# A transformer layer on one core: the second token half is scaled for four tiles at once, turned chunk pair by chunk pair, and the second weight pair's sums move to the end of the turns

## The chip, the core and the metric

The kernel runs on one core of a Trainium2 chip. The metric is device time in microseconds (us) of one execution; a lower time is better. The engines are TensorE (PE in the profile, with PEld for its weight loads), VectorE (DVE), ScalarE (ACT), GpSimd (POOL) and SyncE (SP), whose queue issues the DMA transfers.

## The reference

One layer works on a token block `x` of 1024 tokens by 1024 features, in fp32:

```python
h = _rmsnorm(x, ffn1_norm[i]);  x = x + 0.5 * _swiglu(h, ffn1_w1[i], ffn1_w3[i], ffn1_w2[i])
h = _rmsnorm(x, mix_norm[i]);   proj = h @ w_in[i]      # q, f, v, output gate, pool, two branch gates
...                             # a chunked gated recurrence, a causal multi-scale pool, two branches
y = sigmoid(ga_r) * y_a + sigmoid(gb_r) * y_b;          x = x + y @ w_out[i]
h = _rmsnorm(x, ffn2_norm[i]);  x = x + 0.5 * _swiglu(h, ffn2_w1[i], ffn2_w3[i], ffn2_w2[i])
gate = sigmoid(_rmsnorm(x, ple_norm[i]) @ ple_w_gate[i]);  x = x + gate * e
return _rmsnorm(x, final_norm)
```

Three of the four large stages begin in the same way: all 1024 tokens are normalised, their features are brought onto the partitions, and a wide weight matrix multiplies them (`w1` and `w3` of both feed-forward blocks, and `w_in`). The fourth normalisation belongs to the gate at the end (PLE below).

## The kernel before

**Products.** fp32 operands are split into a high and a low fp32r part: the high part is a cast on ScalarE, the low part a subtraction on VectorE (`split`, L118 and L119). A product of two such operands is three matmuls into one PSUM bank (`mm3`, L157 to L159). A large product is cut into 2 by 2 blocks (token halves on one side, weight halves on the other) and done with seven block products instead of eight. `pair` does this for two weight blocks `wa` and `wb`: products 1 and 2 need only the first token half (B11 and B21, tiles x0h, x0l), product 3 needs B22 (the tile `x`, high and low in one), and products 5, 6 and 7 need T1, T2 and T3 (tiles xT1h, xT1l, xT3h, xT3l), sums of both halves. A block product has 4 chunks of 128 features, so 12 matmuls of 128x512.

On the weight side, `sums` builds S1 to S4 and A22. Four operations on GpSimd do it (L90 and three of L93), with casts on ScalarE and subtractions on VectorE between them: wsh, wsl for S1 and S2; wd for A22; wth, wtl for S3 and S4. The fourth GpSimd operation overwrites the tile `rb`, so it waits until wd has read it.

**The second token half.** `norm_act` brings a stage's tokens onto the partitions. `first` and `second` do it for tiles 0 to 3 and 4 to 7. In `second`, `scales` forms 1/rms of each token: two squares with row sums on ScalarE for each tile (L242), their sum on VectorE (L243), a power on GpSimd (L244) and a diagonal 128x128 matrix on VectorE (L245). This chain is run tile by tile. A *turn* of one chunk is four matmuls against these diagonals into one bank (L255): scaling and transposition in one. Then come the gain (L293, ScalarE) and the split of an odd chunk, and `act_second` (L198, L199, two subtractions L84, casts and subtractions) for a pair of chunks, which makes one chunk of T1, T2, T3 and N4.

In `second` all four odd chunks are turned first, which gives all of B22. Only then the four even chunks follow, each with its `act_second`.

**Leads.** At the start of a stage, `run_pair` collects three weight pairs (the *leads*, 0 to 2) and steps through them and through `second` in a written-out order, so that products 1 and 2 of three pairs and product 3 of two pairs cover the turns. `late` puts a pair's sums behind its products 1 and 2 instead of ahead of them (with a second load of `wa` as `ra`). Each engine takes its instructions strictly in its queue's order. That order is made once, ahead of time, by a scheduler from the order of the code and what depends on what; `tc.issue_after` holds following instructions back behind a given one.

The stages that start this way are FFN1 (its turns fall into about 20 to 70 us of the profile), the mix projection (about 713 to 752 us), and FFN2 (about 1656 to 1705 us). The PLE gate (about 2327 to 2336 us) uses `scales` too. In FFN1 the order is simpler (`begun` is empty): all of `second` runs between the products 1 and 2 of lead 1 and those of lead 2, with the products of the embedding projection (pw, L683) between the chunk pairs.

## Time and profile before

| | before |
|---|---|
| median of 3 runs | 2416.18 us (2415.89 to 2421.88) |
| the profiled execution's own time | 2417.04 us |
| its span, first to last instruction | 2415.3 us |
| mean granted TensorE clock | 0.990 |
| TensorE busy | 2330.6 us, 96% |
| VectorE, ScalarE, GpSimd busy | 1471.4, 980.0, 444.8 us |
| DMA, mean over the span | 137 GB/s |

A row of the timeline gives the start and the duration in us, the engine, the line, the operation, out<-in, how many instructions are in the row, and, in brackets, how long the engine was idle ahead of it and what released it. Matmuls overlap, so the distance between two starts, not the duration, is what one costs. A turn is a pass of eight (x8), since each fp32 matmul is recorded as two. A row of the windows gives a stretch of the span, its length, and for each engine named the busy time and the number of instructions; PEclk is the granted clock as a share of full speed.

### The profile page before, as it was taken

The numbers are of one execution on the slowest core, as the hardware profiler recorded it, in microseconds if no ns is written. First come the engines' busy times: TensorE is split into PE (matmuls) and PEld (weight loads), VectorE is DVE, ScalarE is ACT, GpSimd is POOL, SyncE is SP. The second block draws the span as 40 slices with busy tenths as digits, with TensorE's granted clock in tenths as the row PEclk, the third lists the DMA queues.
The fourth block names the chain that finished last, engine by engine and source line by source line (L and its number), as shares of the span: only waits on it lengthen the run. The fifth ranks groups of instructions, "written<-read, shape, count | busy, mean of one in ns | idle before, by whom it ended". The sixth has DMA issues, their size and how long they took to land. (4 is left out here: it accounts for less than half of the span.)

```text
span 2415.3 us, 29471 instructions
## 1 busy us (share of the span) xinstructions
PE 2330.6 (96%) x11058; PEld 1916.1 (79%) x11058; DVE 1471.4 (61%) x2037; ACT 980.0 (41%) x1528; POOL 444.8 (18%) x397
## 2 busy tenths in 40 slices
PE   8999999999998999999999999999899999999997
PEld 6778888888877888788888877877687888888886
DVE  6555554567656766766566566676544544568568
ACT  6344333333554333333333343237333333334556
POOL 1332223200011222122222102102222222100000
PEclk9999999999999999999999999999999999999999
DMA  4344453484332232222222257652234533663334
GB/s 183 127 143 168 156 174 132 153 322 128 117 114 70 79 96 83 75 88 79 83 81 86 88 189 247 229 207 105 87 129 146 177 102 110 215 251 127 97 100 152
DMA packets 133759, 331.75 MB, mean 137 GB/s; under 512 B 15216, under 2 KB 16240, under 8 KB 133616
## 3 DMA queue, kind: packets, MB, share of 16 engines
q1 hardware_dynamic: 133616, 329.87, 40.1%
q8 instruction: 87, 1.43, 0.3%
q14 instruction: 56, 0.46, 0.1%
HBM read 228.62 MB, written 101.19 MB: 137 GB/s over the span
## 5 line engine op out<-in xcount | busy, mean ns | idle before, releaser
L90 POOL TENSOR_TENSOR s<-rb 128x512 f32<-128x512 f32 x74 | 98.5, 1331 | 780.1 <-DMA rb<-in_ffn_w_dram 352.6
L119 DVE TENSOR_TENSOR wtl<-rb,wth 128x1024 fp32r<-128x1024 f32 x74 | 90.7, 1225 | 152.7 <-ACT wth L118 152.7
L118 ACT CAST wsh<-s 128x1024 fp32r<-128x1024 f32 x74 | 77.8, 1052 | 229.6 <-POOL s L93 215.5
L119 DVE TENSOR_TENSOR wsl<-s,wsh 128x1024 fp32r<-128x1024 f32 x74 | 91.3, 1233 | 117.9 <-ACT wsh L118 117.9
L93 POOL TENSOR_TENSOR rb<-ra,s 128x512 f32<-128x512 f32 x74 | 96.7, 1306 | 349.0 <-DVE wd L119 335.6
L118 ACT CAST wth<-rb 128x1024 fp32r<-128x1024 f32 x74 | 77.7, 1049 | 183.8 <-POOL rb L93 183.8
L954 PEld LDWEIGHTS aux<-qk 128*128 128x128 f32 (+1 forms) x896 | 109.7, 186 | 37.9 <-issue 11.5
L118 ACT CAST gh<-gr 128x1024 fp32r<-128x1024 f32 x84 | 81.8, 980 | 141.8 <-PE aux L158 86.4
L119 DVE TENSOR_TENSOR wal<-ra,wah 128x1024 fp32r<-128x1024 f32 x74 | 91.5, 1238 | 75.1 <-PE pC L158 45.0
L119 DVE TENSOR_TENSOR gl<-gr,gh 128x1024 fp32r<-128x1024 f32 x84 | 95.0, 1134 | 68.2 <-ACT gh L118 68.1
L157 PE MATMUL pA<-xT3h,wth 128*128 128x512 f32 x296 | 119.7, 404 | 8.9 <-ACT g L382 6.8
L954 PE MATMUL aux<-qk 128*128 128x64 f32 (+1 forms) x896 | 110.5, 267 | 17.2 <-DVE qk L87 11.5
L118 ACT CAST wah<-ra 128x1024 fp32r<-128x1024 f32 x74 | 77.6, 1050 | 117.6 <-DMA ra<-in_ffn_w_dram 97.2
L157 PE MATMUL pA<-xT1h,wsh 128*128 128x512 f32 x280 | 114.1, 408 | 10.4 <-ACT xT1h L118 7.1
L157 PE MATMUL pB<-xT1h,wsh 128*128 128x512 f32 x296 | 119.3, 403 | 2.6 <-DVE g L81 1.3
L157 PE MATMUL pA<-x0h,wah 128*128 128x512 f32 x296 | 118.5, 400 | 1.2 <-DVE gb L87 0.7
L157 PE MATMUL pC<-x0h,wah 128*128 128x512 f32 x296 | 118.9, 402 | 0.0
L157 PE MATMUL pB<-x,wth 128*128 128x512 f32 x296 | 118.8, 401 | 0.0
L158 PE MATMUL pA<-x0l,wah 128*128 128x512 f32 x296 | 115.8, 391 | 1.6 <-DVE x0l L119 1.6
L158 PE MATMUL pB<-xT1l,wsh 128*128 128x512 f32 x296 | 116.6, 394 | 0.8 <-DVE xT1l L119 0.8
L157 PE MATMUL pA<-xT3h,wd 128*128 128x512 f32 x280 | 112.8, 403 | 4.3 <-ACT c L385 2.5
L159 PE MATMUL pA<-xT3h,wtl 128*128 128x512 f32 x296 | 116.4, 393 | 0.5 <-DVE wtl L119 0.5
(341 smaller groups left out, 6602.1 us busy)
## 6 DMA issues: line engine op xcount, KB each, us to landing
ra<-in_ffn_w_dram SPq DMA_DIRECT2D x47, 512.0 KB, 3.7
rb<-in_ffn_w_dram SPq DMA_DIRECT2D x44, 512.0 KB, 3.7
gsS<-gs SPq DMA_DIRECT2D x88, 256.0 KB, 2.2
rB<-in_ffn_w_dram SPq DMA_DIRECT2D x40, 512.0 KB, 7.0
gr<-gsS SPq DMA_DIRECT2D x40, 512.0 KB, 3.4
gsA<-g SPq DMA_DIRECT2D x66, 256.0 KB, 2.0
gr<-gsA SPq DMA_DIRECT2D x30, 512.0 KB, 5.9
ra<-in_w_in_dram SPq DMA_DIRECT2D x27, 512.0 KB, 3.6
```

The costliest lines, as they stand in the source:

```text
L90: nc.gpsimd.tensor_tensor(o, x, y, ALU.add)
L93: nc.gpsimd.tensor_tensor(o, x, y, ALU.subtract)
L118: nc.scalar.copy(hi, src)
L119: nc.vector.tensor_tensor(lo, src, hi.bitcast(F32), ALU.subtract)
L157: nc.tensor.matmul(ps, ah, bh, start=first, stop=False, **kw)
L158: nc.tensor.matmul(ps, ah, bl, start=False, stop=False, **kw)
L159: nc.tensor.matmul(ps, al, bh, start=False, stop=last, **kw)
L954: nc.tensor.matmul(ps[:m, c, :64], kc[c][:, :m], right, start=True, stop=True)
```

## The change

`scales` takes the eight squares of four tiles into one statistics tile of 128x8, forms the four sums in one instruction, the four powers in one instruction, and then the four diagonals. `second` goes pair by pair: it turns chunk kc, then chunk kc+1, scales the odd chunk into a 128x512 tile of its own, and calls `act_second`, which now makes the high and low part of B22 too. In `run_pair`, of the three leads only lead 0 has product 3 early, and it comes behind the last turn. The sums of leads 1 and 2 now both stand behind their products 1 and 2 (so lead 1 loads `wa` twice, one more 512 KB transfer in each of two stages). Those of lead 1 also stand behind `mark`, a GpSimd operation on one column that reads the high part of T1's third chunk. `defer` moves the closing addition of product 1 and the reader of C11 behind a step.

```diff
+        if not whole:
+            ss = stat("ss", 8, 2).rearrange("p (k t) -> p k t", k=2)
+            rs = stat("rs", 4, 2)
+            for i, t in enumerate(ts):
                 for k, c in ((1, R), (0, L)):
                     sq = t_("h", "sq")
-                    nc.scalar.activation(sq, x[t][:, c], AF.Square, accum_out=ss[:, k : k + 1])
-                nc.vector.tensor_scalar(rs, ss[:, 0:1], ss[:, 1:2], D * EPS, ALU.add, ALU.add)
-            pow_last[0] = nc.gpsimd.tensor_tensor(rs, rs, mhalf[:, :1], ALU.pow).ins
+                    nc.scalar.activation(sq, x[t][:, c], AF.Square, accum_out=ss[:, k, i : i + 1])
+            nc.vector.scalar_tensor_tensor(
+                rs, ss[:, 0, :], D * EPS, ss[:, 1, :], ALU.add, ALU.add
+            )
+            nc.gpsimd.tensor_tensor(rs, rs, mhalf[:, :4], ALU.pow)
...
-            b22 = []
-            for kc in range(1, KC, 2):
...
-                nc.scalar.mul(b22[kc // 2], turned_by(x, ts, diag, kc), g[:, kc : kc + 1])
-                act["B22"].append(hilo_half(b22[kc // 2], "a", "x3"))
-            yield True
             for kc in range(0, KC, 2):
+                yield True
                 p12 = turned_by(x, ts, diag, kc)
-                act_second(act, b1[kc], b1[kc + 1], p12, b22[kc // 2], g[:, kc : kc + 1],
-                           ng[:, kc : kc + 1])
-                yield True
+                b22 = t_("h", "b22")
+                nc.scalar.mul(b22, turned_by(x, ts, diag, kc + 1), g[:, kc + 1 : kc + 2])
+                act_second(
+                    act, b1[kc], b1[kc + 1], p12, b22, g[:, kc : kc + 1], ng[:, kc : kc + 1]
+                )
                 if beside:
+                    yield True
                     beside(kc)
...
+    def mark():
+
+        t = last_act[0]["T1"][2][0][:, :1].bitcast(F32)
+        return nc.gpsimd.tensor_tensor(lmax[:, :1], t, t, ALU.add).ins
...
-        late = not begun or len(leads) == LEADS - 1
-        third = bool(begun) and len(leads) < LEADS - 1
-        leads.append(pair(*args, **kw, lead=True, late=late, third=third, raws=raws))
+        n = len(leads)
+        leads.append(pair(*args, **kw, lead=True, late=not begun or n > 0,
+                          third=bool(begun) and n == 0, defer=bool(begun) and n > 0, raws=raws))
...
-        steps(second, 1)
-        with tc.issue_after(pow_last[0]):
-            steps(leads[1], 1)
+        steps(second, 2)
         steps(leads[1], 2)
         steps(second, 1)
+        steps(leads[2], 2)
+        steps(second)
         steps(leads[0], 1)
-        steps(second, 1)
-        steps(leads[2], 2)
-        steps(second, 1)
-        steps(second)
-        steps(leads[1], 1)
+        with tc.issue_after(mark()):
+            steps(leads[1], 1)
```

**How the order moves, first place: VectorE at the start of FFN2.** Rows give line, operation, out<-in and shape; wsl, wd and wtl are the first weight pair's, rs the four tokens' scales, `t` the tiles T1 and T3 before their split, and `x_2255` to `x_2260` low parts of B22. Before:

```order
L119 TENSOR_TENSOR wd_12708<-rb_12699,wd_12708 128x512
L243 TENSOR_SCALAR rs_12719<-ss_12718 128x1
L245 TENSOR_SCALAR diag_12717<-ident,rs_12719 128x128
L119 TENSOR_TENSOR wtl_12714<-rb_12699,wth_12713 128x1024
L243 TENSOR_SCALAR rs_12728<-ss_12727 128x1
L245 TENSOR_SCALAR diag_12717<-ident,rs_12728 128x128
L243 TENSOR_SCALAR rs_12737<-ss_12736 128x1
L245 TENSOR_SCALAR diag_12717<-ident,rs_12737 128x128
L243 TENSOR_SCALAR rs_12746<-ss_12745 128x1
L245 TENSOR_SCALAR diag_12717<-ident,rs_12746 128x128
```

Now:

```order
L119 TENSOR_TENSOR wd_12689<-rb_12680,wd_12689 128x512
L241 SCALAR_TENSOR_TENSOR rs_12700<-ss_12699 128x4
L246 TENSOR_SCALAR diag_12698<-ident,rs_12700 128x128 x4
L119 TENSOR_TENSOR wtl_12695<-rb_12680,wth_12694 128x1024
L81 TENSOR_TENSOR g_12656<-g_12656,pA_12723 128x512
L198 SCALAR_TENSOR_TENSOR t_2242_12764<-tr_12752,gains,b_2181_12525 128x512
L199 SCALAR_TENSOR_TENSOR t_2243_12765<-tr_12752,ngains,b_2240_12757 128x512
L119 TENSOR_TENSOR x_2244_12768<-b_2240_12757,x_2244_12768 128x512
```

One sum and four diagonals now stand where four sums and four diagonals took turns with the power on GpSimd, and wtl stands behind all of them; the first L198 now follows at once, where before four low parts of B22 and the second pair's wsl, wd and wtl stood between.

**Second place: GpSimd at the start of FFN2.** `s` and `rb` are the sums of lead 0, 1 and 2 in this order. Before:

```order
L93 TENSOR_TENSOR rb_12699<-ra_12681,s_2228_12701 128x512
L244 TENSOR_TENSOR rs_12719<-rs_12719,mhalf 128x1
L244 TENSOR_TENSOR rs_12728<-rs_12728,mhalf 128x1
L244 TENSOR_TENSOR rs_12737<-rs_12737,mhalf 128x1
L244 TENSOR_TENSOR rs_12746<-rs_12746,mhalf 128x1
L90 TENSOR_TENSOR s_2264_12823<-rb_12821 128x512
```

Now:

```order
L93 TENSOR_TENSOR rb_12680<-ra_12662,s_2220_12682 128x512
L244 TENSOR_TENSOR rs_12700<-rs_12700,mhalf 128x4
L426 TENSOR_TENSOR lmax<-xT1h_12885 128x1
L90 TENSOR_TENSOR s_2286_12947<-rb_12945 128x512
L93 TENSOR_TENSOR s_2286_12947<-s_2286_12947,ra_12943 128x512
L93 TENSOR_TENSOR rb_12945<-ra_12943,rb_12945 128x512
```

One power takes the place of four, and the sums of lead 1 now wait, behind the mark, for the third chunk of xT1h.

**Third place: the DMA queue of SP in FFN1**, from the third weight pair's load on. `gsA` and `gsS` are stores of finished blocks of the up projection, `gp` a gain. Before:

```order
L149 DMA rb_1079<-in_ffn_w_dram 128x1024
L153 DMA gsA_0_23_150<-g_523 128x512
L149 DMA ra_1201<-in_ffn_w_dram 128x1024
L153 DMA gsA_0_29_156<-g_523 128x512
L153 DMA gsS_0_35_162<-gs_386_1125 128x512
L153 DMA gsS_0_41_168<-gs_387_1126 128x512
L153 DMA gsS_0_47_174<-gs_388_1127 128x512
L153 DMA gsS_0_53_180<-gs_389_1128 128x512
L149 DMA rb_1207<-in_ffn_w_dram 128x1024
```

Now:

```order
L149 DMA rb_1069<-in_ffn_w_dram 128x1024
L149 DMA ra_1191<-in_ffn_w_dram 128x1024
L153 DMA gsA_0_23_150<-g_523 128x512
L149 DMA rb_1197<-in_ffn_w_dram 128x1024
L153 DMA gsA_0_29_156<-g_523 128x512
L153 DMA gsS_0_35_162<-gs_382_1115 128x512
L153 DMA gsS_0_41_168<-gs_383_1116 128x512
```

The fourth pair's `rb` stood behind five stores and stands behind one now.

40 lines of the change are left out of this document (23 added, 17 removed).

## The prediction

> **What bounds the kernel now.** I read the page's busy shares first, then a table of stretches, then TensorE's timeline in the stretches that stand out, and last the rows of the engines that release it there.
>
> ```profile
> PE 2330.6 (96%) x11058; PEld 1916.1 (79%) x11058; DVE 1471.4 (61%) x2037; ACT 980.0 (41%) x1528; POOL 444.8 (18%) x397
> ```
>
> TensorE is the bound: 2415.3 - 2330.6 = 84.7 us of the whole span are idle. The change takes no matmul away, so all it can win is part of these 84.7 us and of the time at a lower clock. The stretches that hold the three starts of stages, for PE, PEld, DVE, ACT and POOL in this order:
>
> ```profile
> 60.00:100.00 40.00, 36.81 (x161) 29.18 (x160) 20.55 (x24) 16.47 (x23) 15.45 (x11) 0.96 0.30 103
> 100.00:180.00 80.00, 74.36 (x324) 60.12 (x323) 44.93 (x59) 30.80 (x49) 24.41 (x20) 1.00 0.46 149
> 690.00:800.00 110.00, 102.07 (x484) 83.24 (x483) 72.04 (x102) 49.77 (x75) 28.05 (x23) 0.97 0.28 95
> 1650.00:1750.00 100.00, 90.58 (x408) 71.12 (x408) 61.84 (x82) 46.51 (x73) 22.56 (x20) 0.98 0.24 79
> ```
>
> PE is idle for 3.2, 5.6, 7.9 and 9.4 us in them, 26.1 in all, and in three the granted clock is below 1.00. That is the pot. No other engine is busy for over two thirds of any: what is missing is order, not capacity.
>
> **FFN2, where most is lost.** TensorE, from product 1 of lead 0 to the first matmul of product 7:
>
> ```profile
> 1656.40 0.39 PE L157 MATMUL pA<-x0h,wah 128*128 128x512 f32 x1
> ...
> 1661.61 0.39 PE L159 MATMUL pC<-x0h,wal 128*128 128x512 f32 x1
> ...
> 1664.77 0.94 PE L255 MATMUL tr<-diag,x 128*128 128x128 f32 x6 [0.59 <-DVE diag L245]
> ...
> 1668.22 0.94 PE L255 MATMUL tr<-diag,x 128*128 128x128 f32 x6 [0.83 <-DVE diag L245]
> ...
> 1683.57 1.95 PE L255 MATMUL tr<-diag,x 128*128 128x128 f32 x16
> 1685.27 0.48 PE L157 MATMUL pB<-x,wth 128*128 128x512 f32 x1
> ...
> 1696.27 0.50 PE L157 MATMUL pA<-xT1h,wsh 128*128 128x512 f32 x1 [3.07 <-ACT xT1h L118]
> ...
> 1698.12 0.63 PE L159 MATMUL pA<-xT1h,wsl 128*128 128x512 f32 x1
> 1698.55 0.63 PE L158 MATMUL pB<-xT1l,wsh 128*128 128x512 f32 x1
> ...
> 1701.66 0.50 PE L157 MATMUL pA<-xT1h,wsh 128*128 128x512 f32 x1 [1.05 <-ACT xT1h L118]
> ...
> 1704.66 0.50 PE L157 MATMUL pA<-xT3h,wth 128*128 128x512 f32 x1
> ```
>
> The first two rows are 23 matmuls apart: 5.21 / 23 = 0.2265 us each. The x16 row is two turns, 1.70 us to the next start, so 0.85 a turn. The stretch holds 11 block products (132 matmuls, 29.9 us) and 8 turns (6.8), 36.7 us of work, but takes 1704.66 - 1656.40 = 48.3. So **11.6 us** are lost: waits for the diagonals, then for the last two chunks of xT1h, and behind the 3.07 us wait matmuls 0.43 apart, which is half the rate. Who is late:
>
> ```profile
> 1661.23 1.05 ACT L118 CAST wth<-rb 128x1024 fp32r<-128x1024 f32 x1 [4.55 <-POOL rb L93]
> 1662.18 0.63 ACT L242 ACTIVATE sq<-x 128x512 f32<-128x512 f32 x1
> 1659.92 1.28 POOL L93 TENSOR_TENSOR rb<-ra,s 128x512 f32<-128x512 f32 x1 [13.43 <-DVE rs L243]
> 1681.76 0.75 DVE L198 SCALAR_TENSOR_TENSOR t<-tr,gains,b 128x512 f32<-128x512 f32 x1
> 1687.15 0.74 DVE L198 SCALAR_TENSOR_TENSOR t<-tr,gains,b 128x512 f32<-128x512 f32 x1
> 1701.64 1.23 DVE L119 TENSOR_TENSOR xT1l<-t,xT1h 128x1024 fp32r<-128x1024 f32 x1 [0.39 <-ACT xT1h L118]
> ```
>
> ScalarE sat 4.55 us on wth's cast with six squares queued behind it; and VectorE's chain of pairs, 5.39 us each, begins at 1681.76, because even chunks are turned only after all odd ones. In the new queue the squares stand ahead of that cast. From the adds that end the stage before, I get the last square at about 1660.3. GpSimd then does the fourth sum (1.28) and one power, and the diagonals stand between 1662 and 1662.7, just when products 1 and 2 of lead 0 end (1661.8): 0.3 us of waiting. The first turns end at 1663.8, the first L198 can start at about 1664. A pair now carries one more low part (x, 0.6): 6.0 us. The third chunk of xT1h comes near 1682 (was 1696), the fourth near 1688 (was 1701.5). TensorE's new waits there: 1.6 us for the low part of B22's fourth chunk, which product 3 now reads right behind the last turn; 0.8 for the one bank pB, which product 5 must get from product 3's copy; 0.2 at the third chunk, and 0.5 where product 7 waits until product 6 is added to the copy of product 3. With the 0.3 that is 3.6 us. I take 4.6, since lead 1's wsh now queues on ScalarE behind the fourth chunk's xT3h. **Gain 11.6 - 4.6 = 7.0**; ends 3.0 (two of the four waits return and the clock halves again) and 11.6.
>
> **Mix projection.** The same schedule, with less lost:
>
> ```profile
> 715.91 2.42 PE L255 MATMUL tr<-diag,x 128*128 128x128 f32 x18 [0.64 <-DVE diag L245]
> 741.70:751.80 10.10, 7.19 (x23) 0.83 0.15 43
> 747.94 0.80 PE L157 MATMUL pA<-xT1h,wsh 128*128 128x512 f32 x1 [2.47 <-ACT xT1h L118]
> 727.41 0.74 DVE L198 SCALAR_TENSOR_TENSOR t<-tr,gains,b 128x512 f32<-128x512 f32 x1
> 781.48 0.64 PE L933 MATMUL aux<-ident,v 128*128 128x128 f32 x4 [2.47 <-DMA v<-v_dram]
> ```
>
> 23 matmuls in 10.1 us: 10.1 - 23 x 0.2265 = 4.9 lost, and 0.64 ahead of the turns: 5.5. The diagonals come 1.9 us earlier by the removed rounds, the first L198 12 us earlier (about 715). New waits as above, 2.0 in sum here, since the fourth chunk is later wanted than in FFN2. **Gain 3.5**; ends 0 and 5.5. Later, TensorE waits 2.47 us for v, a load that SP's queue holds behind the next pair's `ra`, and that behind GpSimd's fourth sum of lead 2. Sums that begin earlier release it earlier; the wait and seven matmuls at half rate (7 x 0.2) are 3.9. Lead 2's `rb` now waits for lead 1's fourth sum, so I count half, **1.9**; ends 0 and 3.9.
>
> **FFN1.** Turns, then lead 0's second-half products, then two later pairs:
>
> ```profile
> 21.96 0.91 PE L255 MATMUL tr<-diag,x 128*128 128x128 f32 x6 [2.42 <-issue]
> 24.17 1.03 ACT L118 CAST wah<-ra 128x1024 fp32r<-128x1024 f32 x1
> 65.77 1.58 POOL L90 TENSOR_TENSOR s<-rb 128x512 f32<-128x512 f32 x1 [40.56 <-PE pB L158]
> 72.33 0.39 PE L157 MATMUL pA<-xT1h,wsh 128*128 128x512 f32 x1
> ...
> 74.23 0.50 PE L159 MATMUL pA<-xT1h,wsl 128*128 128x512 f32 x1 [0.84 <-DVE wsl L119]
> 80.21 0.50 PE L157 MATMUL pA<-xT3h,wth 128*128 128x512 f32 x1 [1.14 <-ACT wth L118]
> 81.47 0.50 PE L159 MATMUL pA<-xT3h,wtl 128*128 128x512 f32 x1 [0.53 <-DVE wtl L119]
> 86.15 0.50 PE L157 MATMUL pA<-xT3h,wd 128*128 128x512 f32 x1 [0.67 <-ACT c L385]
> 127.26 0.47 PE L157 MATMUL pA<-xT1h,wsh 128*128 128x512 f32 x1 [2.24 <-DVE g L81]
> 154.62 0.50 PE L157 MATMUL pA<-xT3h,wth 128*128 128x512 f32 x1 [2.46 <-ACT g L382]
> 112.07 0.33 SPq L149 DMA_DIRECT2D rb<-in_ffn_w_dram  x1
> ```
>
> Here the merged scales cost. Before, TensorE turned the first tile at 21.96, while squares went on; now no diagonal stands before all squares are done (24.17, where ScalarE goes on to wah) plus sum, power and diagonal, about 25.4. VectorE's unbroken chain of low parts behind them starts about 1.0 us later, and TensorE follows it: **loss 1.0**; ends 0 and 2.7 (six us of idle time and a slow clock behind it). Lead 0's sums wait for the tile of an earlier product of the embedding (at about 64 instead of 65.77), and wsl and wd stand ahead of T1's and T3's last parts. By the same replay wth is cast at 76 instead of 79 and wtl is there at 78, before it is wanted. The waits 0.84, 1.14, 0.53 and the half rate behind them go. The 36 matmuls from 72.33 to 86.15 took 13.8 us for 8.2 of work; 0.6 stays, the copy c: **gain 5.1**, ends 3.0 and 5.7. For the fourth pair, `rb` was issued at 112.07 behind five stores, and stands behind one now: its sums, then wtl and g on VectorE, ended the 2.24 wait, and in the same way the 2.46 wait at 154.62. 4.7 in all; since gains pass from one pair to the next only as far as their tiles are free, I count half, **2.4**, ends 0 and 4.7.
>
> **PLE.** The wait for the diagonals,
>
> ```profile
> 2328.13 1.60 PE L255 MATMUL tr<-diag,x 128*128 128x128 f32 x12 [0.47 <-DVE diag L245]
> ```
>
> goes: its squares now stand ahead of four bank copies on ScalarE. **Gain 0.5**, ends -1 and 1.
>
> Costed at nothing: the smaller number of sums, powers and instructions (VectorE and GpSimd are not the bound), and the second `ra` of lead 1, 512 KB in two stages. By the row below it is about 3.7 us in a stretch whose DMA share is 0.24 to 0.28, and it is issued some 10 us ahead of its use. Without that cover it would hold lead 1's sums by as much.
>
> ```profile
> rb<-in_ffn_w_dram SPq DMA_DIRECT2D x44, 512.0 KB, 3.7
> ```
>
> **The sum.** 7.0 + 3.5 + 1.9 - 1.0 + 5.1 + 2.4 + 0.5 = 19.4 us. The profiled execution took 2417.04: 2397.6. The median of the runs shown is 0.86 lower: **2396.8 us**.
>
> A rule bears on the 1.0: the Trainium skill, "TensorE: Matmul & The Clock Gate" (What's actually happening), says that an idle window of about 3.4 us halves the clock, and that some 3.4 us of busy time restore it. The trace agrees with the halving, though here 2.47 and 3.07 us of waiting were enough. By the rule the six idle us ahead of the first new turn would put 3.4 us of dense work at half rate, up to 1.7 us more, and the sum would be 2398.5.
>
> **Rivals.** *The wait only moves* (chance 0.15). The pair chain is VectorE's 6.0 x 4 = 24 us; if the first L198 starts late all the same (the gain copy or a table load on ScalarE ahead of the first b22), the T chunks come some 5 us earlier instead of 13. Then mix and FFN2 win 1 and 3, and v nothing; FFN1's sums win 3.0 less the 1.0: 6 us, 2410, with the half of it just inside no change. For it: in the trace ScalarE is late wherever a cast stands ahead. Against: the order puts nothing new ahead of L198.
>
> *Lead 1's sums come too late* (0.08): slower. They wait for the mark. If the third chunk of xT1h came no earlier than in the trace (1696.27), three sums (3 x 1.28), a cast and a low part (1.05, 1.23) would set lead 1's wsl to about 1702.4, 1.0 us after it is wanted. Lead 2's `rb` may be issued only after the fourth sum (low part of A22 0.7, sum 1.28), lands 3.7 later, and needs sums, cast and low part again (6.1): 11.8 us against the 41 matmuls (9.3) in between. 1.0 + 2.5, and half rate behind it (1.4), with casts that stand behind (2): 6.9 us a stage, 13.8 in two. With FFN1's 6.5 that makes 2424. It decides as soon as the mark is later than about 1690 in FFN2.
>
> *More than I count* (0.07): all halves become wholes and the new waits stay hidden, 27 to 31 us, 2387.
>
> *It does not do what it says*: the queues of all engines show the new order, so this gets no chance of its own.
>
> **How the numbers follow.** The forecast has 0.70, with its own range 2389 to 2406 (the terms' ends do not fall together). About 0.3%, 7.2 us, is what a measurement of this kernel can tell from no change, so faster means below 2408.9, slower above 2423.4. The first rival lies half on either side: faster 0.70 + 0.07 + 0.02, and 0.01 off the forecast's tail, 0.78; within 0.3% 0.15; slower 0.07. The range, 2388 to 2412, leaves out the slower rival and the best few cases.
>
> **What would show it.** In the new profile: squares of FFN2's second half ended by 1661, no wait for diag above 0.4 us there; the first L198 within 3 us of the first turn; no wait for xT1h over 1 us, and no matmuls 0.43 apart in mix and FFN2; one new wait for the low part of x and one for the copy of pB; in FFN1 the first turn at about 25.5, no wait for wsl, wth, wtl near 75 to 82, and `rb` of the fourth pair issued before the gsS stores. Wrong it is if wsh or wsl of lead 1 becomes the longest wait in mix or FFN2, or if the wait for v stays at 2.5 while the sums come earlier.

## The result, and the profile after

The changed kernel takes **2405.01 us** (median of 9 runs, 2395.38 to 2410.35) against 2416.18 us of the kernel before, measured beside it (9 runs, 2411.67 to 2422.28). The ratio is **0.9948, 95% interval 0.9935 to 0.9961**: faster by about 12 us, where 19.4 were forecast. The profiled execution took 2405.17 us (before: 2417.04), so the traces differ by 11.9 us, and this difference is what is divided up below. Two later executions far above all others (3922.22 us of the version with the merged scales alone, 8233.16 us of the kernel before) are left out of medians and ratios.

The busy shares on the page of the changed kernel:

```profile
PE 2326.4 (97%) x11058; PEld 1919.8 (80%) x11058; DVE 1475.6 (61%) x2023; ACT 983.8 (41%) x1528; POOL 449.2 (19%) x387
```

TensorE is idle for 77.0 us of a span of 2403.4 us; it was 84.7. Its busy time fell by 4.2 us, with the same matmuls.

To see where the time went, I take first matmuls of a product 1, which every pair has once. Six of them cut the program into stages. TensorE's timeline before:

```profile
196.59 0.39 PE L157 MATMUL pA<-x0h,wah 128*128 128x512 f32 x1
...
708.11 0.39 PE L157 MATMUL pA<-x0h,wah 128*128 128x512 f32 x1
...
839.05 0.40 PE L157 MATMUL pA<-x0h,wah 128*128 128x512 f32 x1
...
1542.41 0.39 PE L157 MATMUL pA<-x0h,wah 128*128 128x512 f32 x1
...
1749.46 0.39 PE L157 MATMUL pA<-x0h,wah 128*128 128x512 f32 x1
...
2077.13 0.39 PE L157 MATMUL pA<-x0h,wah 128*128 128x512 f32 x1
```

The same six matmuls in the changed kernel:

```profile
191.29 0.39 PE L157 MATMUL pA<-x0h,wah 128*128 128x512 f32 x1
...
703.09 0.39 PE L157 MATMUL pA<-x0h,wah 128*128 128x512 f32 x1
...
830.26 0.40 PE L157 MATMUL pA<-x0h,wah 128*128 128x512 f32 x1
...
1534.93 0.39 PE L157 MATMUL pA<-x0h,wah 128*128 128x512 f32 x1
...
1735.87 0.39 PE L157 MATMUL pA<-x0h,wah 128*128 128x512 f32 x1
...
2066.68 0.39 PE L157 MATMUL pA<-x0h,wah 128*128 128x512 f32 x1
```

The lead over the kernel before is 5.30 us at the first, then 5.02, 8.79, 7.48, 13.59 and 10.45, and 11.9 at the end. By stages, with the forecast beside them:

| stage (time before) | lead gained, us | forecast, us |
|---|---|---|
| FFN1, to 197 | +5.3 | 6.5 (-1.0 + 5.1 + 2.4) |
| rest of FFN1, 197 to 708 | -0.3 | 0 |
| mix projection with the wait for v, 708 to 839 | +3.8 | 5.4 (3.5 + 1.9) |
| rest of mix, 839 to 1542 | -1.3 | 0 |
| end of mix and start of FFN2, 1542 to 1749 | +6.1 | 7.0 |
| rest of FFN2, 1749 to 2077 | -3.1 | 0 |
| end, with PLE | +1.5 | 0.5 |
| sum | 11.9 | 19.4 |

Two things stand out. Each stage that the change touches gained, all but the last somewhat less than forecast. And 4.7 us were given back in stretches whose code the change does not touch, which the forecast had at nothing.

At the starts of mix and FFN2, TensorE's timeline in the changed kernel (the third row is FFN2's first product):

```profile
734.16 0.79 PE L158 MATMUL pB<-x,wth 128*128 128x512 f32 x1 [2.92 <-DVE x L119]
...
774.25 0.63 PE L946 MATMUL aux<-ident,v 128*128 128x128 f32 x4 [0.99 <-DMA v<-v_dram]
...
1647.99 0.39 PE L157 MATMUL pA<-x0h,wah 128*128 128x512 f32 x1
...
1680.16 0.79 PE L158 MATMUL pB<-x,wth 128*128 128x512 f32 x1 [2.92 <-DVE x L119]
...
1682.06 0.80 PE L157 MATMUL pB<-xT1h,wsh 128*128 128x512 f32 x1 [0.68 <-ACT g L385]
1682.65 0.63 PE L158 MATMUL pB<-xT1l,wsh 128*128 128x512 f32 x1
1683.07 0.63 PE L159 MATMUL pB<-xT1h,wsl 128*128 128x512 f32 x1
...
1687.98 0.40 PE L157 MATMUL pA<-xT3h,wth 128*128 128x512 f32 x1
```

The long waits for xT1h (2.47 and 3.07 us) are gone, but product 3 waits 2.92 us in both stages for the low part of B22's fourth chunk, where 1.6 us was forecast, and behind it matmuls stand 0.43 us apart again. What VectorE and GpSimd did just then:

```profile
1676.64 1.80 DVE L119 TENSOR_TENSOR xT3l<-t,xT3h 128x1024 fp32r<-128x1024 f32 x1
1678.36 1.75 DVE L119 TENSOR_TENSOR x<-b,x 128x512 fp32r<-128x512 f32 x1
1680.03 2.48 DVE L84 TENSOR_TENSOR t<-b,t 128x512 f32<-128x512 f32 x2
...
1684.12 1.22 DVE L119 TENSOR_TENSOR xT3l<-t,xT3h 128x1024 fp32r<-128x1024 f32 x1
1676.07 1.29 POOL L90 TENSOR_TENSOR s<-rb 128x512 f32<-128x512 f32 x1
1677.43 2.13 POOL L93 TENSOR_TENSOR s<-s,ra 128x512 f32<-128x512 f32 x1
1679.52 1.72 POOL L93 TENSOR_TENSOR rb<-ra,rb 128x512 f32<-128x512 f32 x1
```

The mark has just released lead 1's three sums. Read the ends: the first sum ends at 1677.36, xT3l at 1678.44, the second sum at 1679.56, the low part of x at 1680.11, the third sum at 1681.24, the two L84 at 1682.51. Each instruction ends 1.1 us (0.6 for each 512-wide one on VectorE) behind the last one of the *other* engine, as if the two took turns. Last, a wait in a stretch that the change does not touch, with GpSimd's first sum for that pair and the load of `rb` that this sum reads (the last number is the time from issue to landing, in us):

```profile
1811.61 0.50 PE L157 MATMUL pA<-xT3h,wth 128*128 128x512 f32 x1 [2.11 <-ACT g L393]
1806.82 1.28 POOL L90 TENSOR_TENSOR s<-rb 128x512 f32<-128x512 f32 x1 [13.25 <-PE pA L159]
...
rb<-in_ffn_w_dram SPq DMA_DIRECT2D x1, 512.0 KB, 4.6
```

The same three rows before:

```profile
1823.63 0.50 PE L157 MATMUL pA<-xT3h,wth 128*128 128x512 f32 x1 [0.57 <-ACT g L382]
1818.84 1.29 POOL L90 TENSOR_TENSOR s<-rb 128x512 f32<-128x512 f32 x1 [11.71 <-DMA rb<-in_ffn_w_dram]
...
rb<-in_ffn_w_dram SPq DMA_DIRECT2D x1, 512.0 KB, 3.7
```

The wait grew by 1.5 us, and the load took 0.9 us longer.

### The profile page after: what moved, and what is told of

The parts are those of the page before. It is cut to its first block, busy times and chain, and to the rows that moved or that the text cites. A ratio compares the mean times of both kernels' runs of the same rounds, so it can differ in the third digit from the quotient of the medians.

```text
span 2403.4 us, 29433 instructions
## 1 busy us (share of the span) xinstructions
PE 2326.4 (97%) x11058; PEld 1919.8 (80%) x11058; DVE 1475.6 (61%) x2023; ACT 983.8 (41%) x1528; POOL 449.2 (19%) x387
## 5 line engine op out<-in xcount | busy, mean ns | idle before, releaser
L967 PEld LDWEIGHTS aux<-qk 128*128 128x128 f32 (+1 forms) x896 | 110.5, 188 | 38.5 <-issue 11.4
L158 PE MATMUL pB<-x,wth 128*128 128x512 f32 x296 | 116.2, 393 | 5.8 <-DVE x L119 5.8
L157 PE MATMUL pB<-x,wth 128*128 128x512 f32 x296 | 118.6, 401 | 0.0
L159 PE MATMUL pB<-xT1h,wsl 128*128 128x512 f32 x296 | 117.9, 398 | 0.0
L159 PE MATMUL pB<-x,wtl 128*128 128x512 f32 x296 | 116.3, 393 | 0.0
```

The lines of the kernel that those rows point to most:

```text
L157: nc.tensor.matmul(ps, ah, bh, start=first, stop=False, **kw)
L158: nc.tensor.matmul(ps, ah, bl, start=False, stop=False, **kw)
L159: nc.tensor.matmul(ps, al, bh, start=False, stop=last, **kw)
L967: nc.tensor.matmul(ps[:m, c, :64], kc[c][:, :m], right, start=True, stop=True)
```

## The experiments

The last table of this section gives every run by the stages above. Stages with the same code differ by 1 to 2 us between executions, so single stages are read against that. Each ratio is against runs of the kernel before that were measured beside that version; the medians of those runs lie between 2413.8 and 2416.5 us, so versions are better compared by their ratios than by their times.

**The merged scales alone, in the kernel before.**

```diff
 (kernel before)
-                nc.vector.tensor_scalar(rs, ss[:, 0:1], ss[:, 1:2], D * EPS, ALU.add, ALU.add)
-            pow_last[0] = nc.gpsimd.tensor_tensor(rs, rs, mhalf[:, :1], ALU.pow).ins
...
+            nc.vector.scalar_tensor_tensor(
+                rs, ss[:, 0, :], D * EPS, ss[:, 1, :], ALU.add, ALU.add
+            )
+            pow_last[0] = nc.gpsimd.tensor_tensor(rs, rs, mhalf[:, :4], ALU.pow).ins
```

> The kernel before with nothing but the merged scales (one sum, one power for four tiles); turns, leads and sums stand as before. If the merged scales are what the change lives on, this is 8 us or more faster than before. My reading of the two traces is that they nearly cancel: FFN1's first turn of the second half comes at about 25.9 instead of 21.96, and 2.0 us are lost there, partly by a halved clock; the waits for diag in mix (0.64), FFN2 (0.59 and 0.83) and PLE (0.47) go. Sum -0.5 us, so 2413 to 2418 against 2416 for before. The long waits for xT1h in mix (2.5) and FFN2 (3.1) stay, since the order of the turns is the old one.

Measured: 2411.53 us (nine runs), ratio 0.9981 (0.9967 to 0.9995), a little faster than the 2413 to 2418 us that were expected. The turns in FFN1, TensorE's timeline:

```profile
25.61 1.62 PE L265 MATMUL tr<-diag,x 128*128 128x128 f32 x6 [6.44 <-issue]
```

So most of the gain comes from the other parts of the change, and the idle time of over six us ahead of FFN1's turns belongs to the merged scales. In the old order it is made up for later, though: product 6 begins 1.25 us later than before, but at 197 us this version is 1.1 us ahead. The long waits for xT1h stay, as expected (2.00 us in mix, 2.48 in FFN2), but the waits ahead of the turns did not go (1.89 us in mix, 0.82 and 0.65 in FFN2; before 0.64, 0.59 and 0.83).

**Tile by tile in FFN1 only** (`beside` is set there alone), merged elsewhere.

```diff
 (changed kernel)
-            diag = scales(x, ts)
+            diag = scales(x, ts, tiled=bool(beside))
...
+        if tiled:
+            for i, t in enumerate(ts):
+                r = rs[:, i : i + 1]
...
+                nc.gpsimd.tensor_tensor(r, r, mhalf[:, :1], ALU.pow)
+                nc.vector.tensor_scalar(
+                    diag[:, i * P : (i + 1) * P], ident, r, None, ALU.mult
+                )
```

> The changed kernel, but in FFN1 the scales of the second half go tile by tile again (their columns in the merged tiles, so each tile's diagonal needs only its own two squares). If the 6.4 us of idle TensorE ahead of the first turn and the low clock behind it (0.91 in 20 to 60 us) cost what the trace suggests, the first turn is back near 22, the clock in 20 to 60 us is 1.00, the first product 1 of lead 2 begins 2 us earlier, and the whole is 2 us faster than the changed kernel (2403 against 2405). The rival, that this start is bound by VectorE's low parts of x0 and nothing is won, leaves product 1 of lead 2 within 0.5 us of 68.8.

Measured: **2399.78 us, ratio 0.9925 (0.9909 to 0.9942)**, the best ratio of these versions, though its interval still overlaps that of the changed kernel. The turns:

```profile
20.63 0.68 PE L282 MATMUL tr<-diag,x 128*128 128x128 f32 x4 [2.29 <-issue]
21.81 3.67 PE L282 MATMUL tr<-diag,x 128*128 128x128 f32 x12 [0.50 <-DVE diag L246]
```

The idle time falls from 6.43 to 2.79 us, 3.6 us, and TensorE keeps most of it. Eight executions with merged scales and the new order of chunk pairs gained 2.8 to 5.5 us in FFN1 (mean 4.35), four with scales tile by tile 6.4 to 7.8 (mean 7.0). The turns of the first half begin up to 1.4 us apart in these executions; counted from there the means are 3.8 and 6.5. **In the new order merging costs 2.7 us in FFN1.** The expectation that the clock would be back at 1.00 failed: over 20 to 60 us it is 0.91 in both kernels.

**The mark later: on the low part of B22's fourth chunk.**

```diff
 (changed kernel)
-        t = last_act[0]["T1"][2][0][:, :1].bitcast(F32)
+        t = last_act[0]["B22"][3][1][:, :1].bitcast(F32)
```

> The changed kernel with the mark reading the low part of B22's fourth chunk instead of the high part of T1's third: lead 1's sums on GpSimd start behind that low part. TensorE's order is the same. Theory contention: in the changed kernel GpSimd's three sums run beside VectorE's last subtractions and stretch them (1.22 to 1.80, 0.68 to 1.75), so the low part of B22's fourth chunk is 1.7 us late and TensorE waits 2.92 us for it, long enough to halve the clock behind. Then here that wait falls to about 1.2 us, no matmuls run at half rate there, each of mix and FFN2 is 3.5 us shorter, and the whole is about 7 us faster (2398). Theory chain length: the wait is there because that low part stands behind xT3l and L199 in VectorE's queue, with or without the sums; then the wait stays at 2.5 or more and the later sums make the kernel 0 to 3 us slower (2405 to 2408).

Measured: 2402.41 us, ratio 0.9938 (0.9923 to 0.9952). TensorE and VectorE in FFN2, and TensorE in mix:

```profile
1678.64 0.50 PE L158 MATMUL pB<-x,wth 128*128 128x512 f32 x1 [1.26 <-DVE x L119]
1677.90 0.68 DVE L119 TENSOR_TENSOR x<-b,x 128x512 fp32r<-128x512 f32 x1
...
1683.17 2.31 DVE L119 TENSOR_TENSOR xT3l<-t,xT3h 128x1024 fp32r<-128x1024 f32 x1
743.31 0.50 PE L159 MATMUL pA<-xT1h,wsl 128*128 128x512 f32 x1 [2.09 <-DVE wsl L119]
```

The low part of x is no longer stretched and the wait falls from 2.92 to 1.26, as the theory said. But the time is not the 2398 us that the theory gave, and the stages gained no more (3.3 and 6.1 us). The stretching has only moved on to the instructions behind: from the third chunk's xT3l to the end of the fourth's, VectorE takes 1685.34 - 1676.64 = 8.70 us in the changed kernel and 1685.48 - 1676.77 = 8.71 here. And lead 1's weights now come too late, by 2.09 us in mix.

**The mark earlier: on T1's second chunk.**

```diff
 (changed kernel)
-        t = last_act[0]["T1"][2][0][:, :1].bitcast(F32)
+        t = last_act[0]["T1"][1][0][:, :1].bitcast(F32)
```

> The changed kernel with the mark one chunk earlier (T1's second): the sums start as soon as their weights have landed, about 2.5 to 3.6 us earlier. TensorE's order is the same. Theory contention: all of the stretching (about 2.7 us) now falls ahead of the low part of B22's fourth chunk, TensorE's wait there grows from 2.9 to 3.5 to 4, and the kernel is 1 to 2 us slower (2406 to 2407). Theory chain length: the wait stays 2.9 and nothing changes, or the earlier weights win up to 1 us.

Measured: 2404.96 us, ratio 0.9946 (0.9929 to 0.9963), as the changed kernel. FFN2:

```profile
1676.55 0.50 PE L158 MATMUL pA<-xT1l,wsh 128*128 128x512 f32 x1 [2.17 <-DVE xT1l L119]
1678.94 0.79 PE L158 MATMUL pB<-x,wth 128*128 128x512 f32 x1 [1.42 <-DVE x L119]
```

The wait is split in two and its sum (3.6 us) does not fall. In these three versions it made no difference that shows in the time where beside VectorE's chain the three sums stand.

**Product 3 in another bank, and no early product 3.** Two edits on the theory that VectorE's last chain sets the pace:

```diff
 (changed kernel, first edit)
         if third:
-            pb = bank("pB")
+            pb = bank("aux")
 (changed kernel, second edit)
-                          third=bool(begun) and n == 0, defer=bool(begun) and n > 0, raws=raws))
+                          third=False, defer=bool(begun) and n > 0, raws=raws))
```

> The changed kernel, but product 3 of the first pair gets the bank aux instead of pB (mix and FFN2), so TensorE can go on with products 6 and 5 on the first three chunks before it needs the last low part of x, and product 5 needs no copy of product 3. Theory (the last chain on VectorE, stretched by GpSimd's sums, is what TensorE waits for): the wait of 2.92 us for x falls to about 1.1, the wait of 0.68 for the copy of pB is gone, part of it comes back as waits for the fourth chunk of xT1h and xT1l (1 to 2 us each stage), and product 7 of lead 0 begins about 1.5 to 2.4 us earlier than 1687.98 in FFN2 and as much in mix: 3 to 5 us in all, 2400 to 2402. Rival (the chain's end alone decides, whatever TensorE does before): the waits only move to xT1l, their sum stays at 3.5 us or more with half rate behind it, and the time stays at 2404 to 2406.

> The changed kernel without the early product 3 of the first pair: it stands behind product 4 again, so behind the last turn TensorE meets products 6 and 5 alone, which need xT1h and xT1l. Theory (TensorE is paced by VectorE's last chain, product 3 is the cover): no wait for x at the last turn, but 18 matmuls (4.1 us) after 1672.7 TensorE waits about 5 to 6 us for the fourth chunk of xT1h in FFN2, at half rate behind it; as product 3 is still owed later, each stage loses 1 to 3 us against the change: 2406 to 2410. Rival (product 3 in the bank pB is what makes the wait): the wait for xT1h stays under 3 us and the time is 2400 to 2404.

Measured: 2403.98 us (ratio 0.9957, 0.9944 to 0.9971) with the bank aux, 2403.65 us (0.9954, 0.9939 to 0.9970) without the early product 3. FFN2 with the bank aux:

```profile
1683.28 0.69 PE L157 MATMUL pA<-xT1h,wsh 128*128 128x512 f32 x1 [2.03 <-ACT xT1h L118]
...
1687.08 0.40 PE L157 MATMUL pA<-xT3h,wth 128*128 128x512 f32 x1
```

and without the early product 3:

```profile
1683.00 0.79 PE L157 MATMUL pA<-xT1h,wsh 128*128 128x512 f32 x1 [5.59 <-ACT xT1h L118]
...
1686.98 0.63 PE L157 MATMUL pA<-xT3h,wth 128*128 128x512 f32 x1
```

The waits came about as the theory foresaw them, but neither time did: 2400 to 2402 and 2406 to 2410 were expected. What stays put is the end of VectorE's chain: the fourth chunk of xT1l ends 36.1 to 36.2 us behind the stage's product 1 in FFN2 and 35.0 to 35.1 in mix, in all three kernels, whether product 3 stands before it, between or behind. In FFN2 product 7 hardly moves either (1687.0 to 1688.0). In mix it begins 2.7 us earlier with either edit (37.8 us behind product 1, against 40.5), and still the stage gained no more (2.9 and 2.6 us, against 3.8): the matmuls that are moved are only owed later. The product that is still owed without the early one covers later waits, so moving it costs little: the stages of mix and FFN2 together gained 7.3 us without it and 9.9 in the changed kernel, a little more than executions differ.

**Lead 1's sums where they stood before.**

```diff
 (changed kernel)
-        leads.append(pair(*args, **kw, lead=True, late=not begun or n > 0,
+        leads.append(pair(*args, **kw, lead=True, late=not begun or n == LEADS - 1,
...
-        with tc.issue_after(mark()):
-            steps(leads[1], 1)
+        steps(leads[1], 1)
```

> The changed kernel without the mark: the sums of the second pair are given to GpSimd and VectorE where they stood before (mix and FFN2), so that their low parts stand among VectorE's first chain instead of behind the last one. Theory (each of these instructions on VectorE delays the chain of pairs): wsl, wd and wtl (1.2 + 0.7 + 1.2 = 3.1 us) and the stretching by GpSimd now fall into the first two chains, the last low part of x ends at about the same time or up to 2 us later than 1680.1 in FFN2, the longest wait there is 3 to 5 us, and the time is 2405 to 2410. Rival (only GpSimd's sums beside the last chain matter): the last chain is not stretched (the low part of x takes 0.68 us, not 1.75), the wait for x is 1.3 us or less, and the time is 2400 to 2403.

Measured: 2406.89 us, ratio 0.9976 (0.9963 to 0.9988). VectorE and TensorE in FFN2:

```profile
1671.13 1.22 DVE L119 TENSOR_TENSOR wsl<-s,wsh 128x1024 fp32r<-128x1024 f32 x1
...
1675.82 1.23 DVE L119 TENSOR_TENSOR wtl<-rb,wth 128x1024 fp32r<-128x1024 f32 x1 [2.26 <-ACT wth L118]
1690.60 0.50 PE L158 MATMUL pB<-x,wth 128*128 128x512 f32 x1 [1.61 <-DVE x L119]
```

Nothing in the last chain is stretched, and still it comes late, because wsl, wd and wtl and a wait of 2.26 us for wth's cast stand between VectorE's first chunk pair and its second. The rival (only the sums beside the last chain matter) is out. The one long wait of 3 to 5 us that was expected did not come; there are several of 1.1 to 1.9 instead. Putting the sums last is worth 3.6 us in mix (0.15 gained here, 3.8 in the changed kernel); in FFN2 the difference, 1.4 us, is within what executions differ by. The profiled execution was the slowest of this version's nine (2411.92 us), so its stages stand below its median.

**A shorter chain.** T3's split of each pair is given out behind the next pair's T1:

```diff
 (changed kernel; the same edit in two other versions)
-        for t, names in ((t1, ("T1", "T2")), (t3, ("T3", "N4"))):
+        def parts(t, names):
             for n_, hl in zip(names, halves(hilo(t, "a", "x" + names[0]))):
                 act[n_].append(hl)
+        parts(t1, ("T1", "T2"))
+        return lambda: parts(t3, ("T3", "N4"))
...
+                owed.append(t3)
+                if len(owed) > 1:
+                    owed.pop(0)()
```

> The changed kernel with one more edit: the split of T3 (cast and low part, wanted by product 7 alone) of each chunk pair is given out behind the next pair's T1, in mix and FFN2, so VectorE's chain to the fourth chunk of xT1l and to the last low part of x is one low part (1.22 us, 1.80 where stretched) shorter. Theory (the end of VectorE's chain sets where product 7 of lead 0 begins, whatever TensorE does before it): the wait for x falls from 2.92 to 1.1 to 1.7 us in both stages, product 7 begins 1.2 to 1.8 us earlier than 1687.98 counted from the start of FFN2, and no new wait over 0.5 us for xT3l comes; 1 to 1.8 us a stage, 2402 to 2403. Rival (the chain is not the bound, the sums of lead 1 and their casts are): the wait moves on to wsl of lead 1 and the time stays at 2405.

Measured: 2401.51 us, ratio 0.9943 (0.9926 to 0.9959). FFN2:

```profile
1678.25 0.50 PE L158 MATMUL pB<-x,wth 128*128 128x512 f32 x1 [1.84 <-DVE x L119]
...
1685.64 0.50 PE L157 MATMUL pA<-xT3h,wth 128*128 128x512 f32 x1 [0.96 <-DVE g L81]
```

The wait fell by 1.1 us in both stages. Product 7 of FFN2 begins 1.5 us earlier when counted from the stage's product 1 (38.5 us behind 1647.13, against 40.0 behind 1647.99), as expected, and a new wait of 0.96 us for the addition L81 stands ahead of it. In mix it is 0.5 us (40.0, against 40.5). Mix and FFN2 together gained 10.3 us, 0.4 more than in the changed kernel.

The edit was also put together with the scales tile by tile in FFN1, and with those and the bank aux; and the last two without it:

> The same edit together with FFN1's scales tile by tile (which alone measured 2399.8, with merged scales in mix and FFN2). If the gains add: 2397 to 2398. If the later stages take the gain back, as they did in other runs: 2399 to 2401.

> All three edits: scales of FFN1 tile by tile, product 3 of the first pair in the bank aux, split of T3 behind the next pair's T1. With the bank the wait for x was 0.89 and that for xT1h 2.03 in FFN2. If the end of VectorE's chain is the bound, both shrink by 1.2 to 1.8 us together and product 7 begins earlier by as much; against 2399.9 without the edit of T3 that gives 2397 to 2398, or 2400 if the wait for lead 1's weights takes its place.

> The edit of the bank aux together with the tile by tile scales of FFN1 (which alone measured 2399.8). If both causes are apart from each other their gains add: 2399.8 less 3 to 5, so 2395 to 2397. If the bank only moves the waits: 2399 to 2400. If the first one's gain is lost to later pairs of FFN1: unchanged at 2400 too, and then product 1 of the third pair still begins at 65.2 us.

Measured: 2400.93 (ratio 0.9937, 0.9916 to 0.9958), 2401.22 (0.9942, 0.9926 to 0.9957) and 2399.92 us (0.9940, 0.9922 to 0.9959). None can be told from FFN1's scales tile by tile alone, so that edit is all I would keep of these.

**The sums without their reads.** The cause itself, that two engines take turns, was tested last.

```diff
 (changed kernel, lead 1 in mix and FFN2)
-            pool_add(s[:, L], rb[:, L], rb[:, R])
-            pool_sub(s[:, R], s[:, L], ra[:, L])
+            nc.gpsimd.memset(s[:, L], 0.5)
+            nc.gpsimd.memset(s[:, R], 0.25)
...
-            pool_sub(rb[:, L], ra[:, L], rb[:, L])
+            nc.gpsimd.memset(rb[:, L], 0.125)
```

> The changed kernel, but lead 1's first three sums in mix and FFN2 (128x512, two tiles read from SBUF) are replaced by GpSimd memsets of the same three tiles with a constant, at the same place behind the mark: this leaves the sums of these two weight pairs out, so their products are of constants; all casts, low parts, the fourth sum and all products stay. Theory (GpSimd and VectorE take turns where both read two tiles from SBUF, each instruction waiting for the other's end): beside the memsets, which read nothing, VectorE's instructions keep their own lengths: xT3l 1.22 instead of 1.80, the low part of x 0.68 instead of 1.75, the two L84 together 1.41 instead of 2.48 us; the wait for x falls from 2.92 to 1.3 us or less in both stages, and the fourth chunk of xT1l comes about 2 us earlier than 1682.98 in FFN2. Rival (any work on GpSimd beside VectorE, or the transfers that land then, stretches it): the durations stay within 0.2 us of the changed kernel's. For the time: if the turns cost 2 us of TensorE's time a stage, about 2401; if lead 1's later weights or the later pairs take it back, 2404 to 2406.

This version leaves the three sums out, so its output is not that of the layer. Measured: 2398.59 us, ratio 0.9938 (0.9922 to 0.9955), less than the 2401 us that was expected. FFN2 on VectorE, GpSimd and TensorE:

```profile
1672.15 1.21 DVE L119 TENSOR_TENSOR xT3l<-t,xT3h 128x1024 fp32r<-128x1024 f32 x1
1673.29 0.68 DVE L119 TENSOR_TENSOR x<-b,x 128x512 fp32r<-128x512 f32 x1
1673.89 1.41 DVE L84 TENSOR_TENSOR t<-b,t 128x512 f32<-128x512 f32 x2
1672.02 0.53 POOL L353 MEMSET s<- 128x512 f32 x1
1674.02 0.50 PE L158 MATMUL pB<-x,wth 128*128 128x512 f32 x1 [1.27 <-DVE x L119]
```

Beside memsets at the same place, VectorE's instructions have their own lengths, and the wait is 1.27 us, as expected to the tenth. From the start of xT3l to the end of the L84 VectorE takes 3.15 us here and 5.87 in the changed kernel: **2.7 us of its chain go to taking turns** with three sums. The cast of xT1h's fourth chunk ends 5.3 us behind that of the third in both stages, where it was 8.2. The stages gained 5.9 and 10.3 us instead of 3.8 and 6.1. The 6.3 us between them are more than the turns alone cost, as far as one execution of each can say, since a memset (0.53 us) is also shorter than a sum (1.29), so lead 1's weights come earlier too.

Lead gained by stage in the profiled executions, us, each against the one profiled execution of the kernel before; "end" is all behind 2077:

| kernel | to 197 | to 708 | to 839 | to 1542 | to 1749 | to 2077 | end | span |
|---|---|---|---|---|---|---|---|---|
| changed kernel | 5.3 | -0.3 | 3.8 | -1.3 | 6.1 | -3.1 | 1.5 | 11.9 |
| merged scales alone | 1.1 | 1.6 | 0.7 | 0.1 | 0.8 | 2.4 | 0.5 | 7.3 |
| FFN1 tile by tile | 7.8 | -0.9 | 4.5 | 0.5 | 4.0 | -1.5 | 1.7 | 16.0 |
| mark later | 3.3 | -0.4 | 3.3 | 2.8 | 6.1 | -1.6 | 1.6 | 15.1 |
| mark earlier | 4.3 | -0.3 | 4.0 | 1.9 | 5.3 | -4.2 | 1.3 | 12.4 |
| product 3 in aux | 4.9 | -1.7 | 2.9 | 1.7 | 6.8 | -0.9 | 1.7 | 15.4 |
| no early product 3 | 3.8 | -0.4 | 2.6 | 2.2 | 4.7 | -0.8 | 1.8 | 13.9 |
| lead 1's sums early | 2.8 | -1.5 | 0.1 | 0.8 | 4.7 | -3.6 | 1.8 | 5.1 |
| T3 late | 4.7 | -1.8 | 4.4 | 2.3 | 5.9 | -1.1 | 0.9 | 15.4 |
| tile by tile, aux | 6.4 | 0.4 | 4.1 | 2.0 | 4.8 | -1.5 | 1.5 | 17.6 |
| tile by tile, T3 late | 6.4 | 1.2 | 4.7 | -2.4 | 5.2 | 0.1 | 1.7 | 16.8 |
| tile by tile, aux, T3 late | 7.5 | -0.5 | 0.9 | 3.5 | 5.7 | -1.4 | 1.1 | 16.9 |
| sums without reads | 5.5 | 0.1 | 5.9 | 1.1 | 10.3 | -3.3 | 1.5 | 21.1 |

## Why the prediction was right and wrong

The sign, the range and the places were right: TensorE is the bound, the gain lies at the four starts of stages, and 2405.0 is inside the forecast's own range of 2389 to 2406, near its upper end. That the stages of mix and FFN2 came near their forecast is luck in part: the waits that the sum priced there fell by far less, and gains that it did not have made up for it. Of the rivals, "the wait only moves" holds in part (3.07 us for xT1h became 2.92 for x), by another cause than it named. The size was 0.6 of the forecast, 7.5 us short: 1.2 in FFN1, 1.6 in mix, 0.9 in FFN2, 4.7 in stretches that the sum did not have, less 1.0 more than forecast at the end.

**Nothing given back: the largest difference by stages.** The sum took it that a lead, once won, lasts. In the stretch behind FFN2's start, one wait grew from 0.57 to 2.11 us (the rows at 1823.63 and 1811.61), with half rate behind it. All twelve versions with the new order but one lost 0.8 to 4.2 us in that stretch, the other gained 0.1; merged scales alone gained 2.4. So the give-back there goes with the new order. Its size, some 2 us by the mean of the twelve, rests on the one profiled execution of the kernel before. There GpSimd's first sum of the pair starts 13.8 us behind the product 1 at 1792.99, where before it was 12.3 us behind that at 1806.58: TensorE came 13.6 us earlier and its weights only 12.0. The load of `rb` shows where they stayed behind: it was issued 9.1 us behind that product 1 instead of 8.5, and landed 4.6 us behind its issue instead of 3.7. This took 4.1 to 4.7 us in all twelve versions with the new order, and the wait was 1.29 to 2.11 us; in the two kernels with the old order it took 3.6 to 3.7, and the wait was 0.56 to 0.57. Why the load takes longer there is not settled; no run here tells it apart. The -1.3 us between 839 and 1542 is within what versions differ by: others have -2.4 to +3.5 there.

**FFN2, 7.0 forecast, 6.1 measured: near by luck.** Of the 6.1, 0.9 was gained ahead of FFN2's first product (the lead is 7.5 us at 1542 and 8.4 there). The stretch that the forecast priced runs from that product to the first matmul of product 7. It now holds 110 matmuls and 8 turns, 31.7 us at 0.2265 and 0.85, and takes 1687.98 - 1647.99 = 40.0. So 8.3 us are lost where 11.6 were before, and 4.6 were forecast: the term gained 3.3. The other 1.9 came behind product 7, where waits of 1.60, 0.58 and 0.59 us in the kernel before became 0.49, 0.40 and 0.23; they were not in the term.

The 8.3 are 0.83 ahead of the first turn, 2.92, 0.68, 2.8 at half rate (twelve matmuls from 1680.16 to 1686.38) and about 1 in small gaps. The forecast had 0.3 ahead of the turns; there the one sum took 0.91 us beside GpSimd's fourth sum and the power of four columns 1.02, where one column took 0.21 and 0.55. It had nothing for half rate.

The chain came as worked out as far as its third chunk: counted from the stage's product 1, its cast was forecast to end 25.6 us behind it (1682 less 1656.40) and ended 26.8 behind. The fourth was forecast at 31.6 and came at 35.0. The step that failed is "A pair now carries one more low part (x, 0.6): 6.0 us", which took VectorE's instructions at their lengths without a neighbour on GpSimd, though the change itself moves three sums beside the last of them. From the third cast to the fourth 8.2 us passed in its place, and 5.3 without the sums' reads; 2.7 us of VectorE's chain go to the turns. (The first three casts came 6.5 and 7.3 us apart, with no sum beside them: VectorE waited for ScalarE and did an addition L81 in between, which the 6.0 left out.) Of "1.6 us for the low part of B22's fourth chunk" 1.26 is the chain and the rest to 2.92 the taking of turns.

**Mix and v, 5.4 forecast, 3.8 measured, but in another place.** Counted in the same way, the stretch from mix's product 1 to product 7 lost 6.8 us before and loses 7.4 now: of the 3.5 nothing was won, since 2.92 us for x, 0.68 and half rate behind them stand where 0.64, 0.38, 2.47 and half rate stood. The gain lies behind product 7. The wait for v fell from 2.47 to 0.99 us, and the half rate behind it (eight matmuls from 781.87 to 785.34, 1.7 us too long) is gone: 3.1 us, where 1.9 was counted. Waits of 0.66 and 0.48 us are gone too. With memsets in place of the sums the whole stage gained 5.9.

**FFN1, 6.5 forecast, 5.3 measured (4.35 in the mean).** "Loss 1.0" was too small: TensorE begins product 6 2.0 us later than before (0.4 to 2.5 in the eight executions), and against scales tile by tile in the same order merging costs 2.7. The first turn itself came where it was put (25.4 forecast):

```profile
25.85 1.62 PE L266 MATMUL tr<-diag,x 128*128 128x128 f32 x6 [6.43 <-issue]
...
74.31 0.39 PE L157 MATMUL pA<-xT1h,wsh 128*128 128x512 f32 x1
...
84.28 0.50 PE L157 MATMUL pA<-xT3h,wd 128*128 128x512 f32 x1 [0.68 <-ACT c L396]
```

Product 6 begins 2.0 us later than before (72.33) and the matmul on wd 1.9 earlier (86.15), so the sums of lead 0 gave 3.9, forecast 5.1; from there to 197 another 3.4 came, forecast 2.4. The waits of 2.24 and 2.46 us that this term was taken from are gone, and a new one of 2.23 stands at 131.32.

The Trainium skill, "TensorE: Matmul & The Clock Gate" (What's actually happening), would have added up to 1.7 us to the 1.0, which makes 2.7, the measured number. Half rate did come behind the 6.43 us: the granted clock over 20 to 60 us is 0.91, where it was 1.00 before. But with 2.29 and 0.50 us of waiting instead of 6.43 it was the same 0.91, so the 2.7 between these two versions are the wait and not the clock.

**PLE, 0.5 forecast, 1.5 measured** for everything behind 2077. The 64 matmuls of the turns now stand in one row instead of in pieces between other products; which part of the 1.0 is theirs was not tested.

**The signs named ahead** came out as follows: first L198 within 3 us, no wait for xT1h over 1 us, none for wsl, wth or wtl near 75 to 82, FFN1's first turn near 25.5, `rb` of the fourth pair ahead of the gsS stores, the wait for v below 2.5: right. No matmuls 0.43 apart in mix and FFN2: wrong, by the wait of 2.92. No wait for diag above 0.4 us: wrong in FFN2. TensorE stands still for 0.83 us ahead of its first turn (1654.42), and VectorE's row of diagonals begins at 1654.03; the profile puts this wait down to TensorE's own product 2, but that ended where the idle time begins.

## What to carry to other kernels

When work is moved to another time, look at what the *other* engine of the pair VectorE and GpSimd does just then: in these traces, where both read two tiles from SBUF they do not overlap, and whichever carries the critical chain pays for each neighbour. A wait that moves from place to place as edits change what TensorE does before it, while one late event stays put (the end of VectorE's last chain here), points at a chain on another engine; shorten that chain. Count lost time over the stretch that was priced, and not the stage alone: here two stages looked nearly right although their priced stretches were not. And a lead won at a stage's start should not be counted in full at the end: eleven of the twelve versions with the new order gave some of it back in the same later stretch.

## What the runs showed of the hardware

GpSimd and VectorE took turns by whole instructions: beside two-tile sums on GpSimd, a subtraction of 128x512 on VectorE took 1.75 us instead of 0.68 and one of 128x1024 1.80 to 2.31 instead of 1.22, and GpSimd's own sums 1.72 and 2.13 instead of 1.29; beside memsets of the same tiles nothing was stretched. VectorE's instructions with one operand in PSUM were not held up: L198 kept its 0.74 us at 1672.50 beside a sum, in the version with the mark earlier, while the L84 behind it took 1.12 instead of 0.68. The Trainium skill, "SBUF — State Buffer" (Who interferes with whom), says that a VectorE instruction with two inputs in SBUF contends with a GpSimd instruction that reads SBUF, and not with one that only writes it; its section "Summary: rules for kernel authors" adds that the second one to issue is blocked until the first has finished. The traces agree in all these numbers.

Waits of 2.11 us (1811.61 in the changed kernel), 2.29 us (FFN1, tile by tile, with 0.50 us a little later) and 2.92 us were enough for TensorE to go on at half rate, though not in the same way each time. In the changed kernel it began at once behind the 2.92 us in FFN2 and lasted 6 us, to 1686.06 (granted clock 0.80 over 1676 to 1693). In the version with FFN1 tile by tile the same wait, of the same length, was followed by half rate only 2.0 us later, for 3.4 us (0.90). The Trainium skill, "TensorE: Matmul & The Clock Gate" (What's actually happening), says that the clock goes by a free-running window of about 3.4 us, and that the number of slow matmuls varies between runs of one kernel for that reason. These two traces agree with that, the second one in the 3.4 us too. The granted clock of the nine runs of the changed kernel goes with their times: 0.991 and 0.992 in the four from 2395.38 to 2401.76 us, 0.988 and 0.989 in the five from 2405.01 to 2410.35. That such waits make this spread would fit these numbers, but no run tested it.
